# A trunk layer in float32: the head forms two products k tile by k tile, differences are taken of the raw input, and the K/V pair of the first gates comes last

## The chip, the cores and the metric

The kernel runs on one NeuronCore of one Trainium2 chip. TensorE (PE) multiplies, VectorE (DVE), ScalarE (ACT) and GpSimd (POOL) do elementwise work, and transfers are issued from the queues of SyncE (SP), ACT and POOL. The metric is the device time of one execution in microseconds. "Before" was timed in three executions, with a median of 1818.45 us (1814.23 to 1820.44), and profiled in a fourth.

## The reference

All data is float32: x is 2048 x 1024, one layer.

```python
shift, scale, gate = split(silu(c) @ w_ada + b_ada)      # 1024 each
u = x * (1 + scale) + shift                               # 2048 x 1024
q, k, v, a_gate, p_in, p_gate, m_a, m_p = split(u @ w_in) # 1024,128,128,1024,1024,1024,1024,1024
a = sliding_window_sink_attention(q, k, v, sinks, bias, mask) * silu(a_gate)   # 16 heads, 2 K/V heads, window 128
a = a @ w_attn_proj
p = group_linear(multiscale_causal_pool(p_in), w_pool_mix) * pool_scale * silu(p_gate)
p = p @ w_pool_proj
y = (sigmoid(m_a) * a + sigmoid(m_p) * p) @ w_out * (1 + gate)
out = layer_norm(2 ** 0.25 * x + y, ln_gain, ln_bias)
```

## The kernel before

**Numbers.** A float32 operand is split in two float32r parts: `hi` is a rounded copy made on ACT, `lo = src - hi` is made on DVE. A product of 128 x 128 by 128 x 512 is three matmuls (`mm3`: hi by hi, hi by lo, lo by hi). The third is the first to read the low part of the weights.

**Seven products instead of eight.** The large projections use a Winograd form of Strassen's scheme. For one half s of the sequence (1024 rows, in two chunks of 512), the moving operand u is cut in four blocks: B11 and B12 are the upper 512 features of the two chunks, B21 and B22 the lower 512. Seven operands, called sets, are kept in SBUF as four k tiles with hi and lo each: B11, T1 = B12 - B11, T2 = B22 - T1, B21, T3 = T2 - B11, B22, T4 = B21 - T2. A `Quad` is a pair of 128-column weight tiles; its `load` brings three quarters, and `sum1`, `mid` and `late` form the weight sums. It needs seven products of 12 matmuls each. `front` does B11 and T1 into two PSUM banks a and b; `back` does T2 (bank c) and B21 (onto a), then T3, B22 and T4. Each product but T4 takes its weights from `pair_split` (`first`, `second`, `third`), which writes two buffers out of the ring `w_set` of four. T4 uses `half_split`.

**Order.** `ring` walks over groups of two quads (one group has one). After each product `tick()` advances a position and runs the steps hung there in `hooks`; `steps(hooks, groups, start, todo)` hangs a list of steps at a tick counted through all groups (14 ticks to a group of two). Calls through `pe`, `act`, `dve`, `pool` and `sp` keep their place in the written order on their engine; calls on `nc.*` may be moved by the scheduler of the program.

**The head** (L1090 to L1228) loads w_ada and the first half of x and forms `mod` (shift and 1 + scale) k tile by k tile: `opening(k)` (16 one-column matmuls, a reduction over 128 x 1024 and an addition on DVE), `modulate_x(k)` on ACT. `middle(k)` makes B11 (k < 4) or B21, and the difference that becomes T1 or T2; `closing(k)` splits T1 or T2 one k tile later. `products(i)` does B11 and T1 of the first group per k tile. The T2 and B21 products of that group wait until `back`; their weights are split at the end of the head. The first group is the K/V pair and one quad of the gate `ag`.

**The first gates** (`first_phase`, L1230): 17 quads (K/V, then the gates ag, pg, ma, mp) in nine groups. The leftover sets T3, B22 and T4 are made at positions 0, 1 and 3 of group 0 (`rest`). Between the products four kinds of side work are hung: `fold_parts` (four times: w_pool_in folded with w_pool_mix, on PE, with weights split into two `w_set` buffers), `sums_to` (the sets of the second half of x, written to memory through `kept_parts`, which splits into tiles of the ring `c`), `gate_modulation`, and `turn` (V turned by PE). `spare` is a ring of two 128 x 1024 buffers, `c` one of five 128 x 512. The places of K (`kk`) and V (`vv`) are scratch in the head and then hold K and V. When the groups are done, `first_q` projects the first 128 columns of q (two times 24 matmuls), and attention begins.

## Time and profile before

| | |
|---|---|
| median of three executions | 1818.45 us |
| the profiled execution | 1809.75 us, its span 1808.0 us |
| PE busy | 1717.0 us (95%), 8248 matmuls |
| DVE, ACT, POOL busy | 1335.4, 905.5, 833.7 us |
| mean granted TensorE clock | 0.986 |

A row of the timeline is: start (us), length (us), engine, line, operation, output<-inputs, shape, count; in brackets the idle time before it and what ended it. All calls through the ordered engines carry line 55, so tile names tell them apart: `set_B` and `set_T` are the sets, `mm` and `lg` the PSUM banks for a, b and c, `t` the differences, `W` and `A` a quad's weights. Rows of waits are: who waited, for what, us in total, times, longest. PE's ends are modelled; starts are what is compared below.

### The profile page before, as it was taken

What the parts mean: (1) busy time and instruction counts of PE and PEld (TensorE: products, weight loads), DVE (VectorE), ACT (ScalarE), POOL (GpSimd) and SP (SyncE); (2) the same over time, 40 slices, a digit from 0 to 9 for tenths busy, and PEclk for the clock granted to TensorE, in tenths of its full rate; (3) what the DMA queues carried; (4) which work ended last, traced back from release to release, by engine and by line L of the source; (5) the groups of instructions that cost most, each with busy time, mean ns of one, the idle gap of its engine ahead of it and who ended that gap; (6) DMA issues with size and microseconds to landing.
All of it is one profiled execution on the core that took longest, in us unless ns stands there. A gap on an engine that the chain in (4) does not pass through costs nothing. (4 is left out here: it accounts for less than half of the span.)

```text
span 1808.0 us, 25116 instructions
## 1 busy us (share of the span) xinstructions
PE 1717.0 (95%) x8248; PEld 1430.8 (79%) x8248; DVE 1335.4 (74%) x2348; ACT 905.5 (50%) x1907; POOL 833.7 (46%) x700
## 2 busy tenths in 40 slices
PE   6799999999999999999999999999989999999996
PEld 6578787878888887777777888888868778877775
DVE  5977776655787777877766467777858897976887
ACT  4543434444777776444444367777724333423441
POOL 2134344440346567534434125456753773475442
PEclk9899999999999999999999999999999999999998
DMA  9255667756454557776776633543876575689442
GB/s 358 91 202 189 236 213 235 247 210 169 128 161 138 174 191 301 261 266 234 254 261 238 249 109 129 175 164 117 295 291 211 201 264 176 227 306 372 151 153 88
DMA packets 164002, 381.31 MB, mean 211 GB/s; under 512 B 19728, under 2 KB 23840, under 8 KB 163872
## 3 DMA queue, kind: packets, MB, share of 16 engines
q1 hardware_dynamic: 150528, 342.17, 54.4%
q0 software_dynamic: 10112, 33.06, 5.3%
q10 hardware_dynamic: 3232, 4.49, 0.9%
q8 instruction: 65, 1.06, 0.2%
q14 instruction: 65, 0.53, 0.1%
HBM read 244.35 MB, written 138.44 MB: 212 GB/s over the span
## 5 line engine op out<-in xcount | busy, mean ns | idle before, releaser
L55 PE MATMUL mm<-set_B,w_set 128*128 128x512 f32 x3240 | 799.9, 395 | 16.2 <-DVE w_set L131 14.7
L55 PEld LDWEIGHTS mm<-set_B,w_set 128*128 128x128 f32 x3240 | 602.6, 189 | 146.6 <-DVE w_set L131 20.7
L55 PE MATMUL lg<-set_T,w_set 128*128 128x512 f32 x2088 | 518.9, 398 | 40.1 <-DVE w_set L131 17.2
L55 PEld LDWEIGHTS lg<-set_T,w_set 128*128 128x128 f32 x2088 | 394.7, 191 | 140.1 <-DVE w_set L131 26.9
L131 DVE TENSOR_TENSOR w_set<-W,w_set 128x1024 fp32r<-128x1024 f32 x162 | 224.8, 1387 | 118.6 <-ACT w_set L315 108.2
L315 ACT CAST w_set<-W 128x1024 fp32r<-128x1024 f32 x162 | 169.5, 1049 | 265.3 <-PE mm L55 143.7
L55 PE MATMUL mm<-set_T,w_set 128*128 128x512 f32 x1080 | 266.2, 394 | 0.0
L55 PEld LDWEIGHTS mm<-set_T,w_set 128*128 128x128 f32 x1080 | 201.2, 189 | 41.7 <-DVE nxt L55 0.2
L283 POOL TENSOR_TENSOR W<-W,A 128x512 f32<-128x512 f32 x56 | 81.3, 1451 | 204.0 <-DVE w_set L131 40.0
L293 POOL TENSOR_TENSOR W<-W 128x512 f32<-128x512 f32 x56 | 82.9, 1481 | 158.4 <-DVE w_set L131 149.7
L287 POOL TENSOR_TENSOR W<-W 128x512 f32<-128x512 f32 x56 | 88.6, 1582 | 129.0 <-DVE w_set L131 104.1
L55 DVE TENSOR_TENSOR o<-pv,o 64x128 f32<-64x128 f32 x256 | 72.4, 283 | 92.6 <-ACT o L55 89.8
L55 ACT ACTIVATE L<-L,nm 128x257 f32<-128x257 f32 (+1 forms) x256 | 127.1, 498 | 8.4 <-DVE nm L55 3.2
L55 DVE TENSOR_TENSOR k_lo<-spare,k_hi 128x512 fp32r<-128x512 f32 x88 | 90.8, 1042 | 39.4 <-ACT k_hi L55 17.7
L55 DVE CUSTOM_DVE_ANT_0 L<-lg,bt,nsink 128x256 f32<-128x256 f32 (+1 forms) x256 | 111.5, 473 | 5.3 <-PE lg L55 1.3
L288 POOL TENSOR_TENSOR W<-W 128x512 f32<-128x512 f32 x56 | 91.1, 1627 | 19.7 <-DMA W<-in_win_dram 16.9
L55 POOL TENSOR_TENSOR w_set<-W,w_set 128x1024 fp32r<-128x1024 f32 x14 | 33.7, 2405 | 137.0 <-ACT w_set L55 96.5
L55 POOL TENSOR_TENSOR p<-nxt,pg 128x512 f32<-128x512 f32 x32 | 41.3, 1292 | 104.4 <-DVE sm L55 104.4
L55 ACT COPY o<-pv 64x256 f32<-64x256 f32 x128 | 47.2, 369 | 82.7 <-PE pv L55 80.4
L55 DVE TENSOR_TENSOR ptl<-pt,pth 128x512 fp32r<-128x512 f32 (+1 forms) x128 | 85.6, 669 | 1.7 <-ACT pth L55 1.6
L55 ACT CAST k_hi<-spare 128x512 fp32r<-128x512 f32 x88 | 53.3, 614 | 56.3 <-POOL spare L55 22.3
L55 PE MATMUL lg<-kk,qs 128*128 128x256 f32 (+1 forms) x512 | 80.5, 279 | 0.0
(206 smaller groups left out, 2429.9 us busy)
## 6 DMA issues: line engine op xcount, KB each, us to landing
W<-in_win_dram SPq DMA_DIRECT2D x68, 256.0 KB, 4.2
w_set<-wmix_d SPq DMA_DIRECT2D x32, 512.0 KB, 5.6
A<-in_win_dram SPq DMA_DIRECT2D x34, 256.0 KB, 4.4
W<-in_win_dram POOLq DMA_DIRECT2D x34, 256.0 KB, 3.6
ag_d<-sig SPq DMA_DIRECT2D x32, 256.0 KB, 3.5
pg_d<-sig SPq DMA_DIRECT2D x32, 256.0 KB, 3.2
ma_d<-sig SPq DMA_DIRECT2D x32, 256.0 KB, 3.8
mp_d<-sig SPq DMA_DIRECT2D x32, 256.0 KB, 4.0
```

The costliest lines, as they stand in the source:

```text
L55: return lambda *args, **kw: self.tc.keep_in_program_order(op(*args, **kw))
L131: engine.tensor_tensor(dst, src, as32(hi), ALU.subtract)
L283: e.tensor_tensor(self.w[:, 1, :], self.w[:, 2, :], self.a22, ALU.add)
L287: e.tensor_tensor(x[:, 1, :], x[:, 1, :], x[:, 0, :], ALU.subtract)
L288: e.tensor_tensor(x[:, 2, :], x[:, 0, :], x[:, 2, :], ALU.subtract)
L293: e.tensor_tensor(x[:, 0, :], x[:, 0, :], x[:, 1, :], ALU.subtract)
L315: a.copy(by_two(hi), raw)
```

## The change

1. `difference(k)` (k < 4) subtracts the raw halves of x ahead of the modulation. T1 is then scale times the difference: `closing` makes its hi by an ACT activation with a scale and its lo by a DVE `scalar_tensor_tensor`, and stores -scale in `sg`. T2's difference for k >= 4 is `t * (-scale) + B22`, one `scalar_tensor_tensor`.
2. `second_pair` and `more` do the T2 and B21 products of the first group inside the head, in parts as their k tiles come. `back` then gets the copy of bank a ready-made and leaves out both products.
3. T3 is made at the end of the head; B22 and T4 at positions 4 and 6 of group 0. `late` of the second quad moves to position 4.
4. In the first gates K/V goes from the first to the last group; the first group is two `ag` quads. V is turned at position 7 of the last group and between the two q projections. `place_kv` takes the places of K and V only then.
5. Until then these places are lent: folds split their weights into `room_k` and no longer into `w_set`; two of every three `kept_parts` split into `room_k`; `spare` takes every second pair from `room_v`.
6. Positions move: folds from 13, 41, 69, 92 to 11, 39, 67, 91, with one more tick between each split and its fold; `sums_to` of tile 0 from 1 to 4; `gate_modulation` by one tick, the last by five less.

```diff
         def __init__(self, name, **bufs):
-            self.name, self.bufs = name, bufs
+            self.name, self.bufs, self.turns = name, bufs, {}
         def __enter__(self):
             self.stack = ExitStack()
...
         def split(self):
             return wp.tile([P, D], F32R, tag="wset", bufs=4, name="w_set")
+        def turn_of(self, ring):
+            return next(self.turns[ring]) if ring in self.turns else None
+
         def spare(self, dt=F32):
+            room = self.turn_of("spare")
+            if room is not None:
+                return room
             return self.t.tile([P, D], dt, tag="spare", bufs=self.bufs["spare"], name="spare")
         def c(self, name="c", dt=F32, tag="c"):
...
         t = []
         def split():
-            t.extend(ph.c(n, F32R) for n in ("k_hi", "k_lo"))
+            at = ph.turn_of("parts")
+            if at:
+                t.extend(cols(rooms["k"], n + 2) for n in at)
+            else:
+                t.extend(ph.c(n, F32R) for n in ("k_hi", "k_lo"))
             act.copy(t[0], src())
             low(dve, t[1], src(), t[0])
...
     def back(ph, grp, opened, nxt, own, tick, b22_first=False):
         st = []
-        for q, (a, b, c, w) in zip(grp, opened):
-            u2, p5 = ph.p("u2"), ph.p("p5")
-            nc.scalar.copy(u2, a)
+        for q, (a, b, c, w, *copy) in zip(grp, opened):
+            u2 = copy[0] if copy else ph.p("u2")
+            p5 = ph.p("p5")
+            if not copy:
+                nc.scalar.copy(u2, a)
             if w is None:
                 w = pair_split(ph, q.second())
                 q.late()
...
             tick()
             nc.vector.tensor_tensor(u2, c, u2, ALU.add)
             nc.vector.tensor_tensor(p5, b, u2, ALU.add)
-            product(a, w[0], "B21")
+            if not copy:
+                product(a, w[0], "B21")
             tick()
             q.consume(ph, 0, 0, a)
             st.append((q, b, c, u2, p5))
...
         def consume(ph, mi, t, src):
             if mi == 0:
+                if s == 0 and t == 0:
+                    place_kv(ph)
                 take_k(s, t, src)
             else:
                 vt = ph.c("vt")
...
     def moving_u():
         return (sets["B11"], sets["B21"]), (sets["T2"], sets["B22"])
-    def first_q(ph, tick):
+    def first_q(ph, turn=None):
         raw, hi, lo = ph.spare(), ph.split(), ph.split()
         nc.sync.dma_start(raw, win[TQ])
...
         for us in moving_u():
             acc, part = projection(us)
             part((hi, lo), 0, KT)
+            if turn and not accs:
+                turn(1)
             accs.append(acc)
         return accs
...
                     m.append(wp.tile([P, CH], F32R, tag="A22", bufs=2, name=n))
                 act.copy(m[0], r[0])
                 low(dve, m[1], r[0], m[0])
-            w[:] = ph.split(), ph.split()
+            w[:] = (cols2(rooms["k"], n) for n in range(2))
             act.copy(w[0], r[1 + half])
             low(dve, w[1], r[1 + half], w[0])
...
             (0, lambda: fetch(0)),
             (1, lambda: fetch(1)),
             (2, lambda: split(0)),
-            (3, lambda: fold(0)),
-            (4, lambda: (keep(), split(1))),
-            (5, lambda: fold(1)),
-            (6, keep),
+            (4, lambda: fold(0)),
+            (5, lambda: (keep(), split(1))),
+            (7, lambda: fold(1)),
+            (8, keep),
         )
     def modulate(u, k):
...
     def gate_quads(s):
         kv, turn = kv_quad(s)
-        quads = [kv]
+        quads = [kv] if s else []
         for name, base, kind in (("ag", TAG, "silu"), ("pg", TPG, "scaled"), ("ma", TMA, ""), ("mp", TMP, "")):
             for m in range(0, KT, 2):
                 quads.append(gate_quad(s, name, base, m, kind))
-        groups = [quads[i : i + 2] for i in range(0, 14, 2)] + [quads[14:15], quads[15:17]]
-        return groups, turn
+        last = quads[15:] if s else [kv, quads[15]]
+        return [quads[i : i + 2] for i in range(0, 14, 2)] + [quads[14:15], last], turn
     def gate_modulation(ph, m, cb):
         wa = []
...
             b1, b2 = xs[k]
             if k < 4:
-                t = ts[k] = ph.p("t")
-                minus(t, b2, b1)
                 pool.dma_start(b12_d[k // 2, :, k % 2, :], b2)
             else:
-                minus(ts[k - 4], b2, ts[k - 4])
+                dve.scalar_tensor_tensor(ts[k - 4], ts[k - 4], sg[:, k - 4 : k - 3], b2, ALU.mult, ALU.add)
             parts("B11" if k < 4 else "B21", k % 4, b1)
+        def difference(k):
+
+            t = ts[k] = ph.p("t")
+            minus(t, xs[k][1], xs[k][0])
+
         def closing(k):
-            parts("T1" if k < 4 else "T2", k % 4, ts[k % 4])
+            if k >= 4:
+                parts("T2", k - 4, ts[k - 4])
+                return
+            hi, lo = sets["T1"][:, k, 0, :], sets["T1"][:, k, 1, :]
+            scale = mod[:, KT + k : KT + k + 1]
+            act.activation(hi, ts[k], AF.Copy, scale=scale)
+            dve.scalar_tensor_tensor(lo, ts[k], scale, as32(hi), ALU.mult, ALU.subtract)
+            act.activation(sg[:, k : k + 1], scale, AF.Copy, scale=-1.0)
         def rest_sums(i):
             minus(xs[i][0], ts[i], xs[i][0])
...
             if k < 2:
                 grp[k].load(ph, False, sp, None)
         opening(0)
+        difference(0)
         modulate_x(0)
         opening(1)
+        difference(1)
         middle(0)
         modulate_x(1)
+        def second_pair(x):
+
+            o, u2 = opened[x], ph.p("u2")
+            o[2:] = bank("lg"), pair_split(ph, grp[x].second(), act, dve), u2
+            act.copy(u2, o[0])
+
+        def more(x, name, i0, i1):
+            a, b, c, w, _ = opened[x]
+            if name == "T2":
+                product(c, w[1], name, True, i0, i1)
+            else:
+                product(a, w[0], name, False, i0, i1)
+
         for k in range(2, KT):
             opening(k)
+            if k < 4:
+                difference(k)
+            if k == 7:
+                second_pair(0)
             closing(k - 2)
             middle(k - 1)
             if k == 2:
...
                     q.sum1(dve)
                     starts.append(pair_split(ph, q.first(), act, dve))
             modulate_x(k)
-            if k in (3, 5):
-                grp[k // 2 - 1].mid(pool, dve)
+            if k in (3, 4):
+                grp[k - 3].mid(pool, dve)
             if 3 <= k < 7:
                 products(k - 3)
             if k > 5:
                 rest_sums(k - 6)
+        more(0, "T2", 0, 2)
+        more(0, "B21", 0, 3)
         closing(6)
+        second_pair(1)
+        more(1, "T2", 0, 2)
+        more(1, "B21", 0, 3)
         middle(7)
-        opened[0][3] = pair_split(ph, grp[0].second(), act, dve)
         closing(7)
-        opened[1][3] = pair_split(ph, grp[1].second(), act, dve)
-        for i in (3, 2):
+        for x in range(2):
+            more(x, "T2", 2, 4)
+            more(x, "B21", 3, 4)
+        for i in (2, 3):
             rest_sums(i)
-        for q in grp:
-            q.late(dve)
-        dve.tensor_scalar(nsink, nsink, -1.0, None, ALU.mult)
         late_sets(cp, "B22")
         late_sets(ph.t, "T3", "T4")
-        parts("T4", 1, xs[5][0])
+        for i in range(4):
+            parts("T3", i, xs[i][0])
+        grp[0].late(dve)
+        dve.tensor_scalar(nsink, nsink, -1.0, None, ALU.mult)
         rest = [
-            lambda name=name, src=src, ks=ks: [parts(name, i, src(i)) for i in ks]
-            for name, src, ks in (
-                ("T3", lambda i: xs[i][0], range(4)),
-                ("B22", lambda i: xs[4 + i][1], range(4)),
-                ("T4", lambda i: xs[4 + i][0], (0, 2, 3)),
-            )
+            lambda name=name, c=c: [parts(name, i, xs[4 + i][c]) for i in range(4)]
+            for name, c in (("B22", 1), ("T4", 0))
         ]
         return groups, turn, opened, cb, rest
...
             hooks.setdefault((group, pos), []).append(f)
         for g in range(4):
-            steps(hooks, groups, (13, 41, 69, 92)[g], fold_parts(ph, g))
-        for i in range(2):
-            at(0, (7, 10)[i], lambda i=i: turn(i))
+            steps(hooks, groups, (11, 39, 67, 91)[g], fold_parts(ph, g))
+        at(-1, 7, lambda: turn(0))
         for j in range(KT):
             at(3 + j // 2, 3 + 5 * (j % 2), lambda j=j: spread_bias(j))
         for i in range(4):
...
                 lambda x, r, ks=ks: modulate(x, ks[r]),
                 True,
             )
-            steps(hooks, groups, (1, 29, 57, 80)[i], todo)
+            steps(hooks, groups, (4, 29, 57, 80)[i], todo)
         for i in range(8):
-            steps(hooks, groups, 28 * (i // 2) + 20 + i % 2, gate_modulation(ph, 2 * KT + i, cb))
-        for n, f in zip((0, 1, 3), rest):
+            steps(hooks, groups, (21, 49, 77, 99)[i // 2] + i % 2, gate_modulation(ph, 2 * KT + i, cb))
+        at(0, 4, lambda: groups[0][1].late(dve))
+        for n, f in zip((4, 6), rest):
             at(0, n, f)
         for half in range(2):
             at(-1, 3 + half, lambda half=half: build(ph, "T2", half, b12_d))
-        return ring(ph, groups, opened, hooks, [], lambda tick: first_q(ph, tick))
+        return ring(ph, groups, opened, hooks, [], lambda tick: first_q(ph, turn))
     def second_phase(ph, opened, groups, turn):
         hooks = {(0, (8, 10)[i]): [lambda i=i: turn(i)] for i in range(2)}
...
                     steps(hooks, groups, 19 + 26.5 * i + 2.6 * n, resplit(ph, *halves_of.pop(0)))
         for half in range(2):
             hooks.setdefault((-1, 3 + half), []).append(lambda half=half: fill_set("T2", half, u1_d["B12"]))
-        return ring(ph, groups, opened, hooks, [], lambda tick: first_q(ph, tick), True)
+        return ring(ph, groups, opened, hooks, [], lambda tick: first_q(ph), True)
     def pairs(make):
         return [[make(m), make(m + 2)] for m in (0, 4)]
+
+    rooms = {}
+    kk = vv = None
+
+    def place_kv(ph):
+
+        nonlocal kk, vv
+        ph.turns.clear()
+        kk = kvp.tile([P, 2, 2, P + 2 * CH], F32R, tag="kk", name="kk")
+        vv = kvp.tile([P, 2 * NB + 1, 2, P], F32R, tag="vv", name="vv")
+
+    def cols2(t, n):
+        return t[:, n * D : (n + 1) * D]
     kv_stack = ExitStack()
     kvp = kv_stack.enter_context(tc.tile_pool(name="kvp", bufs=1))
...
     with Pools("g0", spare=2, p=4, c=5) as ph:
         started = head(ph)
-        kk = kvp.tile([P, 2, 2, P + 2 * CH], F32R, tag="kk", name="kk")
-        vv = kvp.tile([P, 2 * NB + 1, 2, P], F32R, tag="vv", name="vv")
+        rooms["k"] = kvp.tile([P, 4 * (P + 2 * CH)], F32R, tag="kk", name="room_k")
+        rooms["v"] = kvp.tile([P, 2 * (2 * NB + 1) * P], F32, tag="vv", name="room_v")
+        ph.turns["spare"] = cycle([None, None] + [cols2(rooms["v"], n) for n in range(2)])
+        ph.turns["parts"] = cycle([(2, 3), (4, 5), None])
         q0 = first_phase(ph, *started)
     with Pools("a0") as ph:
         gates1 = gate_quads(1)
```

1 line of the change is left out of this document (added).

## The prediction

> **What bounds the kernel now.** I read the page first, then PE's waits by stretch, then the timelines of PE, DVE and ACT in the stretches where PE waits.
>
> ```profile
> span 1808.0 us, 25116 instructions
> PE 1717.0 (95%) x8248; PEld 1430.8 (79%) x8248; DVE 1335.4 (74%) x2348; ACT 905.5 (50%) x1907; POOL 833.7 (46%) x700
> ```
>
> PE works through one fixed order of matmuls, so the change gains just what it takes out of PE's waits and slow clock. PE's waits from 24 to 76 us, then from 100 to 440 us:
>
> ```profile
> PE lg L55 <- DVE w_set L131: 6.3, 1, 6.3
> PE lg L55 <- ACT w_set L55: 3.8, 1, 3.8
> ...
> PE lg L55 <- DVE w_set L55: 1.2, 1, 1.2
> ...
> PE lg L55 <- ACT w_set L315: 7.7, 6, 1.9
> PE lg L55 <- DVE w_set L131: 3.8, 8, 0.5
> PE pv L55 <- DVE w_set L55: 0.8, 1, 0.8
> PE mm L55 <- DVE w_set L131: 0.7, 2, 0.4
> PE pv L55 <- ACT w_set L55: 0.6, 1, 0.6
> ```
>
> There are two places: the end of the head (11.3 us of waits) and the folds (most of 13.6 us). Around the head's end, by stretch (length, then PE, PEld, DVE, ACT, POOL busy, granted clock, DMA):
>
> ```profile
> 28.50:49.10 20.60, 20.57 (x114) 17.91 (x113) 19.17 (x35) 14.81 (x23) 2.16 (x4) 1.00 0.81 318
> 49.10:68.90 19.80, 14.82 (x50) 11.20 (x50) 19.72 (x33) 14.03 (x23) 0.00 (x0) 0.74 0.22 74
> ```
>
> To 49.1 PE is full; from there DVE is, 19.72 us of 19.80. PE and DVE from there on:
>
> ```profile
> 52.85 1.22 PE L55 MATMUL lg<-set_T,w_set 128*128 128x512 f32 x2 [3.77 <-ACT w_set L55]
> 55.27 4.63 PE L55 MATMUL lg<-set_T,w_set 128*128 128x512 f32 x10 [1.21 <-DVE w_set L55]
> ...
> 68.25 0.62 PE L55 MATMUL lg<-set_T,w_set 128*128 128x512 f32 x2
> 75.13 4.63 PE L55 MATMUL lg<-set_T,w_set 128*128 128x512 f32 x10 [6.26 <-DVE w_set L131]
> 79.57 3.57 PE L55 MATMUL mm<-set_B,w_set 128*128 128x512 f32 x12
> ...
> 107.49 2.60 PE L55 MATMUL lg<-set_T,w_set 128*128 128x512 f32 x10 [0.36 <-DVE w_set L131]
> ...
> 114.74 0.94 PE L55 MATMUL lg<-set_T,w_set 128*128 128x512 f32 x2 [1.93 <-ACT w_set L315]
> 116.00 3.71 PE L55 MATMUL lg<-set_T,w_set 128*128 128x512 f32 x10 [0.31 <-DVE w_set L131]
> ```
> ```profile
> 49.11 0.15 DVE L55 TENSOR_TENSOR mod<-mod,lg 128x1 f32<-128x1 f32 x1 [0.18 <-PE lg L55]
> ...
> 54.00 1.22 DVE L55 TENSOR_TENSOR w_set<-W,w_set 128x1024 fp32r<-128x1024 f32 x1
> 55.14 0.68 DVE L55 TENSOR_TENSOR set_T<-t,set_T 128x512 fp32r<-128x512 f32 x1
> 55.74 1.22 DVE L55 TENSOR_TENSOR w_set<-W,w_set 128x1024 fp32r<-128x1024 f32 x1
> ...
> 73.86 1.22 DVE L131 TENSOR_TENSOR w_set<-W,w_set 128x1024 fp32r<-128x1024 f32 x1
> ```
>
> The reader should see three things. The T2 products start only when their weights are split, 3.77 us after PE ran dry. T3's third matmul (75.13) waits for one DVE split, done at 75.08 because DVE has a queue of leftover sets and K copies ahead of it. And after such a gap ten matmuls take 4.63 us, where 2.60 is the full rate.
>
> **The change, part by part. T2 and B21 inside the head.** Start to start on DVE, a 512-wide operation takes 0.60 us and a weight split 1.14 (54.00, 55.14, 55.74). The four raw differences move ahead of the modulation one for one, into iterations where DVE has waits; in the last iterations PE is the limit (full to 49.1), so I leave `opening(7)` where it ends now, at 49.2. From there, in the new order, DVE does: split of the first quad's second weights (to 50.3), T2[1] low (50.9), the two of `middle(6)` (52.1), two leftover sums (53.3), T2[2] low (53.9), the second quad's weights (55.1), `middle(7)` (56.3), T2[3] low (56.9). PE can then run, at 0.23 us a matmul (2.75 from product to product of twelve; the 2.88 of a row holds the last one's tail): quad 0's first 15 matmuls of 24 between 49 and 53.6, waiting for DVE about 1 us; quad 1's first 15 from 55.1 to 58.1; the last 18 by 62.2. Now they end at 68.9.
>
> T3 comes next. DVE goes on with four leftover sums (59.3), four T3 lows (61.7) and `late` (62.3). The T3 weights follow on ACT and DVE; at the earliest at 64.5 (1.05 on ACT, 1.14 on DVE), at the latest behind the six 512-wide operations of `back` for both quads, 67.2. I take 65.4, behind one quad's three. So T3's third matmul moves from 75.1 to 65.4: **-9.7**. B22 and T4 (eight lows, 4.8 us) and the second `late` (0.6) now come later on DVE, under the T3 and B22 products of 2.75 us each. They are hidden by a narrow margin; without that cover they would cost up to 2.4 us each.
>
> The clock: the half rate after 75.13 costs 2.0 + 0.7 = 2.7 us now (4.63 against 2.60, 3.57 against 2.88 for twelve at full rate, a row below). After the change the gap ahead of T3 is some 3 us; its nearest row is 114.74, where 1.93 us of waiting cost (3.71 - 2.60) + 0.2 = 1.3. Net -1.4, of which I give back 1.0 for slow matmuls among the 48: **-0.4**. [...]
>
> The cost on DVE: `scalar_tensor_tensor` with a column as scalar, in SBUF:
>
> ```profile
> L611 DVE SCALAR_TENSOR_TENSOR wide<-wide,carry,wide 128x512 f32<-128x512 f32 x6 | 4.2, 745 | 0.4 <-POOL carry L607 0.4
> ```
>
> That is 0.06 us over a subtraction's 0.68, eight times 0.5 us, mostly while PE is full: nothing. ACT gains four scaled activations and four small ones, under 2 us, where it is busy 14.81 of 20.60 us. The `mid` of quad 1 and its POOL transfer go one iteration earlier; its split is 10 us off.
>
> **Folds without `w_set`.** A typical fold, ACT then PE:
>
> ```profile
> 201.74 1.05 ACT L55 CAST w_set<-spare 128x1024 fp32r<-128x1024 f32 x1 [2.15 <-DMA spare<-in_wpt_dram]
> ```
> ```profile
> 199.53 2.88 PE L55 MATMUL mm<-set_B,w_set 128*128 128x512 f32 x12
> 204.27 0.73 PE L55 MATMUL lg<-set_T,w_set 128*128 128x512 f32 x2 [1.86 <-ACT w_set L315]
> 205.53 2.56 PE L55 MATMUL lg<-set_T,w_set 128*128 128x512 f32 x10 [0.53 <-DVE w_set L131]
> ```
>
> The fold takes two of four buffers, so the next pair can be split only when the B21 product (199.53) is done, and PE waits for the whole split. Groups without a fold show waits of 0.3 to 0.5 us at most. Of the 13.6 us of waits from 100 to 440 us (7.7 + 3.8 + 0.8 + 0.7 + 0.6), four such small ones make 1.6; the eight halves of folds have 12.0, and the slow clock after 114.74 adds 1.3: 13.3 in all. With the folds in `room_k` each pair has two products (5.5 us) to hide 2.2 us of split, a slack of 3.3. What is late next is ACT itself, which stands in order behind the fold's two loads (first two rows, ACT's waits from 75 to 440 us):
>
> ```profile
> ACT w_set L55 <- DMA spare<-in_wpt_dram: 7.6, 4, 3.1
> ACT mhi L55 <- DMA mr<-in_mix_dram: 6.8, 4, 2.5
> ACT k_hi L55 <- DMA u_T_split<-k_hi: 6.6, 2, 4.3
> ```
>
> That is 3.6 us a fold, against 3.3 of slack; the longer `spare` lets the loads go two ticks earlier past fewer stores on SP. I keep 2.0 back: **-11.3**, with bounds -13.3 and -6.
>
> **The last fold** moves one position, behind the T3 product of the single-quad group. Its `mlo` and `mhi` hold the two `A` places that the next group's quads load into:
>
> ```profile
> 379.53 0.86 SPq L277 DMA_DIRECT2D A<-in_win_dram  x2
> ```
> ```profile
> 385.96 1.33 DVE L131 TENSOR_TENSOR w_set<-W,w_set 128x1024 fp32r<-128x1024 f32 x1 [2.86 <-ACT w_set L315]
> ```
>
> From that issue to the finished split are 7.7 us, and now 8.2 us of products cover them (T3, B22, T4); then only two, 5.5. SP's stores behind the load wait too. Price 2.2, less the two matmuls that need no low part: **+1.7** (0 to 4; a gain is excluded, PE's work is the same).
>
> **K/V last.** The same instructions move. In the last group `take_k` puts four casts and four subtractions (some 0.6 us each) per chunk ahead of a pair split with 3.3 us of slack, and V's turn lies between the two q projections (5.5 us each). The nearest row is K/V in the first gates of the second half, where K is taken on the way to this wait:
>
> ```profile
> 740.95 2.60 PE L55 MATMUL mm<-set_B,w_set 128*128 128x512 f32 x10 [0.26 <-DVE w_set L131]
> ```
>
> I take **+0.7** (-0.5, since V's turn leaves a stretch where DVE is full, to 5, all of `take_k` exposed). The lent `room_v` is priced at nothing: no place in it is asked for again before its last user is four ticks past. The pairs in `room_k` come round after three splits, some two ticks or 5.5 us, about what a split and its store take (the longest wait for a store is 4.3, the `k_hi` row); that is part of the 2.0 kept back. The other moved positions change no order on PE beyond the folds', and I price them at nothing.
>
> **Sum**: -9.7 - 0.4 - 11.3 + 1.7 + 0.7 = -19.0 us. Against the profiled execution, 1809.75, that is 1790.8. That execution is 0.5% below the median of 1818.45; on the median's scale, which I predict, **1799**.
>
> **The rivals.** *The folds' ACT waits stay* (0.14): if the loads land no earlier, 3.6 us a fold exceed the slack, and half of 11.3 goes: 1805.
>
> *Half clock through the head's products* (0.11): PE now gets T2 and B21 in crumbs. At the rate of 55.27 (0.44 us a matmul) 48 take 21 us, from 49.4 to 70.5, and T3 gains 4.6, not 9.7: 1804. The stretch 49.10 to 68.90 with its clock of 0.74 speaks for it; that it had 5 us of gaps and not 2 speaks against. [...]
>
> *K/V's chain holds up attention* (0.07): in the head's group, where DVE was full, K and V took 41 us, from 63.0 to 104.3:
>
> ```profile
> 63.01 0.58 ACT L650 CAST kk<-mm 64x512 fp32r<-64x512 f32 x1 [0.98 <-PE mm L55]
> ...
> 103.65 0.74 DVE L131 TENSOR_TENSOR vv<-pt,vv 128x256 fp32r<-128x256 f32 x2
> ```
>
> At the end eight products and two q projections, 33 us, follow the first K. If it were as slow there, 8 us would be exposed: 1806. The row at 740.95 speaks against it.
>
> *One room, one lock*, the slower side (0.12, and 0.07 that it only eats up the gain; this also stands for a cost of its kind that I don't see): if uses of a lent tile wait for each other though they touch different columns, 22 of the 32 splits of `sums_to` wait on ACT for the store before them, 3.3 us each by the `k_hi` row, 73 us in all. About half would lie within the slack; I estimate 30 us on PE, and the folds' gain is lost with it. What is left of the gain is 7.7, so it decides from 8 us on; worked out, 1841. Against it: a load into the third column block of `head_B` was issued while PE still read the first:
>
> ```profile
> 8.07 0.44 SPq L55 DMA_DIRECT2D head_B<-in_wadat_dram  x1
> ```
> ```profile
> 7.82 3.55 PE L55 MATMUL pv<-ct,head_B 128*128 128x1 f32 x16 [7.82 <-DMA head_B<-in_wadat_dram]
> ```
>
> **The numbers.** Forecast 0.49, rivals as given. The forecast's own range adds its bounds: 1791 to 1810. The range, 1788 to 1813, adds what runs differ by and leaves out the last rival's 0.19. A measurement tells apart about 0.3%, 5.4 us: the forecast and the first three rivals are faster (0.81), the last gives 0.07 within and 0.12 slower.
>
> **What would show it.** T2 matmuls should start near 49 to 50 us, all 48 end by 62 to 65, and T3's third matmul start near 65. PE's waits for `w_set` between 100 and 440 us should fall from 13.6 to some 4. Attention should begin some 19 us earlier, and the rest keep its length. I am wrong if waits reappear there under another name: DVE ahead of B22 or T4, `A` ahead of the last group, ACT behind a fold's load, or the clock below 0.9 between 50 and 80 us.

## The result and the profile after

The kernel after takes 1810.94 us (median of nine executions, 1805.66 to 1816.67); before, beside it, the median of nine was 1818.45 us (1811.51 to 1820.44). The ratio is 0.9964, with a 95% interval of 0.9947 to 0.9980: faster by 7.5 us between the medians, 6.5 us by the ratio. The prediction was 19 us. So the sign was right, and more than half of the gain is missing. The profiled execution after took 1813.58 us, span 1811.8 us; the one before, 1809.75 us, lies 0.5% below its median. The two spans can't be set against each other, and I compare the same products in both.

The page's first lines after, and PE's waits after from 24 to 76 us and from 100 to 440 us (who waited, for what, us in total, times, longest):

```profile
span 1811.8 us, 25114 instructions
PE 1716.2 (95%) x8248; PEld 1428.6 (79%) x8248; DVE 1344.2 (74%) x2348; ACT 905.7 (50%) x1911; POOL 841.8 (46%) x700
```
```profile
PE lg L56 <- DVE w_set L132: 2.5, 1, 2.5
PE lg L56 <- ACT w_set L326: 1.6, 1, 1.6
...
PE lg L56 <- DVE w_set L56: 0.8, 1, 0.8
...
PE mm L56 <- DVE w_set L132: 5.8, 6, 1.4
PE lg L56 <- ACT w_set L326: 4.0, 1, 4.0
PE lg L56 <- DVE p L400: 1.5, 1, 1.5
PE lg L56 <- DVE w_set L132: 1.4, 2, 1.0
PE mm L56 <- ACT w_set L326: 1.4, 1, 1.4
```

Ahead of T3, 11.3 us of waits became 4.9. Between 100 and 440 us, 13.6 became 14.1: the same sum under other names. The folds' waits (six for ACT with `lg`, and those of `pv`) are all gone; in their place stand seven waits of `mm` (`set_B` products), three small ones of `lg`, and one of 4.0 us that has no like before. PE's timeline after shows where:

```profile
48.52 0.72 PE L56 MATMUL lg<-set_T,w_set 128*128 128x512 f32 x2
...
63.90 0.73 PE L56 MATMUL lg<-set_T,w_set 128*128 128x512 f32 x2 [1.62 <-ACT w_set L326]
67.12 4.05 PE L56 MATMUL lg<-set_T,w_set 128*128 128x512 f32 x10 [2.49 <-DVE w_set L132]
...
82.31 5.33 PE L56 MATMUL lg<-set_T,w_set 128*128 128x512 f32 x22 [2.41 <-DVE w_set L132]
...
89.10 2.56 PE L56 MATMUL mm<-set_B,w_set 128*128 128x512 f32 x10 [0.99 <-DVE w_set L132]
...
95.62 2.60 PE L56 MATMUL mm<-set_B,w_set 128*128 128x512 f32 x10 [0.79 <-DVE w_set L132]
...
100.78 2.88 PE L56 MATMUL lg<-set_T,w_set 128*128 128x512 f32 x12
...
144.29 2.56 PE L56 MATMUL mm<-set_B,w_set 128*128 128x512 f32 x10 [1.15 <-DVE w_set L132]
...
374.62 0.73 PE L56 MATMUL mm<-set_B,w_set 128*128 128x512 f32 x2 [1.42 <-ACT w_set L326]
375.98 2.57 PE L56 MATMUL mm<-set_B,w_set 128*128 128x512 f32 x10 [0.63 <-DVE w_set L132]
...
396.60 5.47 PE L56 MATMUL lg<-set_T,w_set 128*128 128x512 f32 x12 [4.01 <-ACT w_set L326]
...
421.65 2.71 PE L56 MATMUL mm<-set_B,w_set 128*128 128x512 f32 x11
```

T3's third matmul comes 8.0 us earlier (67.12 against 75.13). The first T2 product of the next group, at 100.78, comes 5.7 us earlier (106.51 before): the waits at 82.31, 89.10 and 95.62, 4.2 us together, took 2.3 net back. It isn't more in part because V's turn, 0.8 us of PE's work and a wait of 0.4 (at 88.52 and 97.81 before), now comes behind this point. From there to T4 of the eighth group the gain grows by 9.0, to 14.7 us; the last fold (374.62, 375.98) takes 2.6, the wait at 396.60 with its twelve matmuls at half rate 6.4, and V's turn 0.4. At the q projections (421.65 against 426.93) 5.3 us are left.

What DVE and POOL do ahead of the waits in group 0, and DVE further on, after:

```profile
65.86 1.22 DVE L132 TENSOR_TENSOR w_set<-W,w_set 128x1024 fp32r<-128x1024 f32 x1
...
75.27 1.78 DVE L56 TENSOR_TENSOR set_T<-head_kk,set_T 128x512 fp32r<-128x512 f32 x1
...
78.67 2.38 DVE L56 TENSOR_TENSOR set_T<-head_vv,set_T 128x512 fp32r<-128x512 f32 x2
...
81.58 1.28 DVE L132 TENSOR_TENSOR w_set<-A,w_set 128x512 fp32r<-128x512 f32 x2
...
83.38 1.52 DVE L56 TENSOR_SCALAR spare<-spare,mod 128x1024 f32<-128x1024 f32 x2
...
128.44 0.69 DVE L408 TENSOR_TENSOR c<-mm,u 128x512 f32<-128x512 f32 x1 [6.09 <-PE mm L56]
...
137.76 2.32 DVE L56 CUSTOM_DVE_ANT_0 spare<-spare,cb,mod 128x1024 f32<-128x1024 f32 x1
...
140.62 1.27 DVE L56 CUSTOM_DVE_ANT_0 spare<-spare,cb,mod 128x1024 f32<-128x1024 f32 x1
```
```profile
73.02 1.78 POOL L294 TENSOR_TENSOR W<-W,A 128x512 f32<-128x512 f32 x1 [32.54 <-DMA A<-in_win_dram]
...
78.28 1.62 POOL L299 TENSOR_TENSOR W<-W 128x512 f32<-128x512 f32 x1
```

T3's weights are split at 65.86, behind all six operations of `back`: the late end that the prediction had worked out. T4's (81.58) come behind T4's own four subtractions, which take up to 1.8 us and not 0.6 while POOL sums the next group's weights. At 128.44 DVE stands 6 us ahead of the first sum that follows a B22 product (tile `c`, L408), and the two reductions of `gate_modulation` now follow each other at 137.76 and 140.62, ahead of the weight split that PE waits for at 144.29.

For the wait at 396.60: first the issues and ACT's wait after, then the stretch from 384 to 396 us (length, PE, PEld, DVE, ACT, POOL busy, granted clock, DMA share, GB/s), then the transfers issued from 380 to 400 us (packets of ACT's queue; KB each and median us to landing), and the usual time from the page:

```profile
382.67 0.40 ACTq L1317 DMA_DIRECT2D gate_d<-mod  x1
384.07 0.57 POOL L300 DMA_DIRECT2D W<-in_win_dram  x1 [0.30 <-POOL W L298]
...
395.51 1.04 ACT L326 CAST w_set<-W 128x1024 fp32r<-128x1024 f32 x1 [9.55 <-DMA W<-in_win_dram]
```
```profile
384.00:396.00 12.00, 8.48 (x36) 6.32 (x35) 1.23 (x1) 1.54 (x2) 1.85 (x2) 0.94 0.23 25
```
```profile
q10 hardware_dynamic: 1040, 0.00, 2.9%
...
W<-in_win_dram POOLq DMA_DIRECT2D x2, 256.0 KB, 7.1
gate_d<-mod ACTq DMA_DIRECT2D x1, 4.0 KB, 9.3
```
```profile
W<-in_win_dram POOLq DMA_DIRECT2D x34, 256.0 KB, 4.1
```

`mod` is stored to `gate_d` as 1024 single elements (4 KB in over a thousand packets). The last quarter of the next quad's weights, issued 1.4 us later, was there only at 395.5, 11.4 us after its issue, where 4.1 is usual; in these 12 us the DMA engines moved 25 GB/s. In the profile before, the same transfer was issued later, where only a DVE operation waited for it (5.5 us, at 425.00):

```profile
411.34 0.43 ACTq L1268 DMA_DIRECT2D gate_d<-mod  x1
```

It came earlier because the change moves the last pair of `gate_modulation` five positions ahead, and the store is a call that goes out as soon as `mod` is complete.

### The profile page after: what moved, and what is told of

Read it like the earlier page. It is cut to its first block, busy times and chain, and to the rows that moved or that the text cites. A ratio compares the mean times of both kernels' runs of the same rounds, so it can differ in the third digit from the quotient of the medians.

```text
span 1811.8 us, 25114 instructions
## 1 busy us (share of the span) xinstructions
PE 1716.2 (95%) x8248; PEld 1428.6 (79%) x8248; DVE 1344.2 (74%) x2348; ACT 905.7 (50%) x1911; POOL 841.8 (46%) x700
## 5 line engine op out<-in xcount | busy, mean ns | idle before, releaser
L298 POOL TENSOR_TENSOR W<-W 128x512 f32<-128x512 f32 x56 | 90.5, 1616 | 142.2 <-DVE w_set L132 110.2
L304 POOL TENSOR_TENSOR W<-W 128x512 f32<-128x512 f32 x56 | 84.6, 1512 | 148.3 <-DVE w_set L132 140.7
L299 POOL TENSOR_TENSOR W<-W 128x512 f32<-128x512 f32 x56 | 93.4, 1667 | 19.9 <-DMA W<-in_win_dram 16.8
L56 DVE TENSOR_TENSOR k_lo<-spare,k_hi 128x512 fp32r<-128x512 f32 x61 | 64.6, 1065 | 31.0 <-ACT k_hi L56 14.8
L56 ACT ACTIVATE L<-L,sm 128x256 f32<-128x256 f32 (+1 forms) x128 | 64.3, 502 | 31.4 <-DVE sm L56 31.2
```

The costliest lines, as they stand in the source:

```text
L56: return lambda *args, **kw: self.tc.keep_in_program_order(op(*args, **kw))
L298: e.tensor_tensor(x[:, 1, :], x[:, 1, :], x[:, 0, :], ALU.subtract)
L299: e.tensor_tensor(x[:, 2, :], x[:, 0, :], x[:, 2, :], ALU.subtract)
L304: e.tensor_tensor(x[:, 0, :], x[:, 0, :], x[:, 1, :], ALU.subtract)
```

## The experiments

One execution of these kernels tells little of the time (before's lay between 1809.8 and 1824.4). So the experiments are read at two points of PE's order: T2 of the second group (106.51 us before, 100.78 after) and the start of the q projections (426.93 and 421.65). Three of them are also timed. Experiments 1 and 11 are one kernel profiled twice, and agree to 0.1 us at the first point (100.94, 101.03) and to 0.4 at the second (415.15, 414.78). What the clock does behind a wait is less steady: ten matmuls behind the last fold took 2.57 us after (375.98), 4.63 in experiment 1 and 4.06 in experiment 11, behind waits of 2.0 to 2.3 us. So a difference of up to 3 us at the q projections counts only together with a wait that is named.

**1. The store of `gate` later.** Is the wait at 396.60 the store's doing, or late work on ACT and DVE? It is moved into attention (n counts its steps).

```diff
-            nc.scalar.dma_start(gate_d.rearrange("k p -> p k"), mod[:, 16:24], allow_slow_non_contiguous=True)
...
+            if s == 0 and n == 20:
+                act.dma_start(gate_d.rearrange("k p -> p k"), mod[:, 16:24], allow_slow_non_contiguous=True)
```

> The changed kernel, but the transfer of the gate row (gate_d<-mod, 1024 pieces of 4 bytes) is issued in attention and no longer between the two quads' last weight quarters of the last group. Theory: that transfer is what held the second quarter (issued at 384.07, used at 395.51). Then PE's wait of 4.01 us and the product at half rate behind it (5.47 us for 2.88) go, and the q projections start near 415 us where they start at 421.65 now. Rival: the K/V work on ACT and DVE in the last group makes that wait; then the wait stays and they start at 421 to 422.

The wait is gone and the q projections start at 415.15, 6.5 us earlier; from 384 to 396 us PE is busy for all 12.00 us at a granted clock of 1.00 (8.48 us and 0.94 after). The theory holds. (Up to the product ahead of that wait this kernel is 0.7 us behind, 387.26 against 386.54, so the store is worth 7.2 us here. The 6.4 above are against the kernel before, which has a wait of 0.5 us of its own at this place.) The profile of this kernel also names what DVE waits for in the row of 128.44 above: the fold's result, which is being stored out of the same ring `c`.

```profile
127.76 0.69 DVE L408 TENSOR_TENSOR c<-mm,u 128x512 f32<-128x512 f32 x1 [5.64 <-DMA wmix_d<-st_hi]
```

**2. `gate_modulation` at its old positions.**

```diff
-            steps(hooks, groups, (21, 49, 77, 99)[i // 2] + i % 2, gate_modulation(ph, 2 * KT + i, cb))
+            steps(hooks, groups, 28 * (i // 2) + 20 + i % 2, gate_modulation(ph, 2 * KT + i, cb))
```

> The changed kernel with gate_modulation at its old positions (20, 48, 76, 104). Theory: its two reductions on DVE now come back to back ahead of the second quad's first split, and make the waits of 1.15 us at 142.5 and 1.35 us at 229.6; these go (2.5 us). With the last pair later, the gate row's transfer also leaves the place between the last weight quarters, 6.6 us: q projections near 412.6. Rival: the leftover work of group 0 and the sums make these waits and the K/V work the last one: 421 to 422, waits as they are.

The last group's wait goes here too (0.6 us is left), but the q projections start at 418.31, not at 412.6. The reductions meet other work; one of them, in DVE's row, now stands ahead of the `p` sum that PE waits for (PE's row):

```profile
133.07 2.28 DVE L56 CUSTOM_DVE_ANT_0 spare<-spare,cb,mod 128x1024 f32<-128x1024 f32 x1
...
136.11 4.38 PE L56 MATMUL lg<-set_T,w_set 128*128 128x512 f32 x12 [3.73 <-DVE p L400]
```

Half right: what the new positions cost in the last group, they had gained elsewhere.

**3. Folds split into `w_set` again.**

```diff
-            w[:] = (cols2(rooms["k"], n) for n in range(2))
+            w[:] = ph.split(), ph.split()
```

> The changed kernel with the folds' weights split into w_set again, all else as changed. Theory: the lent room is worth what the eight waits at the folds were in the kernel before, 12 us of waits: the q projections move from 421.65 to 431 to 435. Rival: with one more tick between split and fold the ring would do as well; then under 3 us, 422 to 425.

The q projections start at 431.25, 9.6 us later than after, and the old waits are back in the groups from 100 to 440 us (the longest of the eight is the store's):

```profile
PE lg L56 <- ACT w_set L326: 10.8, 8, 3.7
```

PE's waits in this stretch add up to 20.2 us, 6.1 more than after. With the spacing of the folds as it is after the change, the lent place is worth 9.6 us. This part of the prediction holds.

**4. The head's products back behind the head.**

```diff
-        more(0, "T2", 0, 2)
-        more(0, "B21", 0, 3)
...
-            more(x, "B21", 3, 4)
+        opened[0][3] = pair_split(ph, grp[0].second(), act, dve)
...
+        opened[1][3] = pair_split(ph, grp[1].second(), act, dve)
```

> The changed kernel with the first group's T2 and B21 products behind the head again; T3 stays in the head, K/V last. Theory: these products in the head are worth the 8 us that T3's third matmul came earlier: it starts at 74 to 76 us again (67.1 now), and the q projections at 428 to 430. Rival: group 0 then waits for DVE in any case, and B22 and T4 are ready while PE is still busy: T3 at 70 to 72 us, and the q projections lose under 3 us, 422 to 425.

T2 of the second group at 101.03 (100.78 after), the q projections at 420.88 (421.65). T3 came earlier than either expectation had it: it starts at 67.71 and doesn't wait. DVE gets to T4's split at 81.49 (81.58 after), and so PE reaches T4 at the same time with and without the products in the head:

```profile
67.71 2.93 PE L56 MATMUL lg<-set_T,w_set 128*128 128x512 f32 x12
...
82.22 6.95 PE L56 MATMUL lg<-set_T,w_set 128*128 128x512 f32 x22 [2.81 <-DVE w_set L132]
```

The rival holds: in this kernel the head's products are worth nothing.

**5. Before, with K/V last and nothing else.**

```diff
-        quads = [kv]
+        quads = [kv] if s else []
...
+        last = quads[15:] if s else [kv, quads[15]]
...
-            at(0, (7, 10)[i], lambda i=i: turn(i))
+        at(-1, 7, lambda: turn(0))
...
+            if turn and not accs:
+                turn(1)
```

> The kernel before with K/V moved to the last group and nothing else: no lent places, no products in the head, the leftover sets as they were. Theory (DVE is the bound from the end of the head to T4 of group 0, and K/V's own work on DVE there is only part of it): three K subtractions stand ahead of T3's split in the profile before (67.88, 69.92, 71.94), some 2 us, so T3's third matmul comes at 73 and not 75.1, T4's first product at 87 and not 88.9, and the q projections start 1 to 2 us earlier, at 425 to 426 (426.9 before). Rival (taking K/V out of group 0 is the whole of what the change gained there): T4 at 82 to 83, q projections at 420 to 421.

```profile
69.37 2.58 PE L55 MATMUL lg<-set_T,w_set 128*128 128x512 f32 x10 [0.63 <-DVE w_set L131]
...
100.70 2.88 PE L55 MATMUL lg<-set_T,w_set 128*128 128x512 f32 x12
...
109.81 5.68 PE L55 MATMUL lg<-set_T,w_set 128*128 128x512 f32 x12 [3.51 <-ACT w_set L315]
```

Neither: T3's third matmul comes at 69.37 (75.13 before), T4 starts at 84.26, between the two, and T2 of the second group at 100.70. That is 5.8 us earlier than before, as much as the kernel after has at this point. My expectation counted only the K subtractions in front of T3's split. On DVE, K (first row) and V had 9.2 us of the profile before between 60 and 110 us (length; PE, PEld, DVE, ACT busy; granted clock, DMA share, GB/s):

```profile
60.00:110.00 50.00, 0.00 (x0) 0.00 (x0) 6.30 (x9) 4.80 (x8) 0.93 0.46 156
...
60.00:110.00 50.00, 0.00 (x0) 0.00 (x0) 2.87 (x5) 1.18 (x2) 0.93 0.46 156
```

The `ag` quad in their place takes 3.1 us more there (its products into `sig`: 6.94 against 3.81), so DVE is relieved of some 6 us. T3's split runs at 68.10 and not 73.86. Of these 5.8 us, the four K subtractions that stood ahead of it are 2.7; most of the rest is order, since a `p` sum and three subtractions of T3 now come behind that split. And 1.2 of the 5.8 us at T2 are V's turn with its wait, which moved on PE itself. The next fold, still in `w_set`, then waits longer (109.81, 3.5 us and half rate), and at the q projections 2.0 us are left (424.96).

**6. The next group's weights later (no verdict),** with the store of `gate` late. Moving the loads one or two products later in `back` was to bring POOL's sums behind T4's subtractions.

```diff
+            n = len(opened[0]) > 4 and (2 if q is nxt[0] else 1)
-            defer(1, lambda: q.load(ph, own, e=None))
-            defer(3, lambda: q.sum1(nc.gpsimd))
+            defer(1 + n, lambda: q.load(ph, own, e=None))
+            defer(3 + (n > 0), lambda: q.sum1(nc.gpsimd))
```

> The kernel after with the transfer of gate late (as in the first experiment), and in group 0 the loads of the next group's weights asked for one or two products later, so that POOL's four sums come behind T4's subtractions on DVE. Theory (DVE's five operations from 74.6 to 81.0 take 6.4 us and not 3.0 because POOL works beside them, 73.0 to 79.9): they take 3 us again, T4's first product starts at 79.5 to 80 (82.5 in the first experiment), and the q projections 2 to 3 us earlier, at 412 to 413 (415.15). Rival (DVE is slow there for another reason, or has too much to do anyway): T4 at 82 to 83 and the q projections at 415 or later.

These loads are calls that the scheduler may move, and POOL's sums still began at 72.3. T4 at 82.58 and the q projections at 414.36 tell nothing of the theory; experiment 10 asks again.

**7. Folds at their old positions**, still in the lent place, with the store of `gate` late.

```diff
-            (4, lambda: fold(0)),
-            (5, lambda: (keep(), split(1))),
-            (7, lambda: fold(1)),
-            (8, keep),
+            (3, lambda: fold(0)),
+            (4, lambda: (keep(), split(1))),
+            (5, lambda: fold(1)),
+            (6, keep),
...
-            steps(hooks, groups, (11, 39, 67, 91)[g], fold_parts(ph, g))
+            steps(hooks, groups, (13, 41, 69, 92)[g], fold_parts(ph, g))
```

> The kernel after with the transfer of gate late, and the folds at their old positions with their old spacing (starts 13, 41, 69, 92; split and fold in neighbouring positions), still split into the lent place. Theory (the new waits at 128 and 134 and the two ahead of the last group come from the moved fold steps): the 2.05 us ahead of the last group and the 1.5 at 134 go, the q projections start at 411 to 412 (415.15 in the first experiment). Rival (the wider spacing is what hides the folds' loads and splits): PE waits for the folds' splits, 0.5 to 1.5 us in each of eight halves, and the q projections start at 417 or later.

The waits ahead of the last group go, but the q projections start at 419.26, 4.1 us later than in experiment 1: PE now waits for the folds' splits, 4.5 us in four waits.

```profile
358.88 0.39 PE L56 MATMUL pv<-mhi,room_k 128*128 128x256 f32 x1 [1.89 <-ACT room_k L56]
```

The rival holds, with one limit: positions and spacing were moved together. One of the two, and by these waits the spacing, is part of what makes the lent place pay.

**8. T4's subtractions one position earlier (with the store of `gate` late), and five repairs at once.**

```diff
-        for n, f in zip((4, 6), rest):
+        for n, f in zip((4, 5), rest):
```

The second kernel has this, the store of `gate` late, and three more: the reductions of a pair three positions apart, the second half of a fold stored out of the lent place, and the last fold's second half one position earlier.

```diff
-            steps(hooks, groups, (21, 49, 77, 99)[i // 2] + i % 2, gate_modulation(ph, 2 * KT + i, cb))
+            steps(hooks, groups, (21, 49, 77, 99)[i // 2] + 3 * (i % 2), gate_modulation(ph, 2 * KT + i, cb))
...
-                st = [ph.c(n, F32R).rearrange("p (m e d) -> p m e d", m=2, e=2) for n in ("st_hi", "st_lo")]
+                st = [cols(rooms["k"], 2 * n + i) if lent else ph.c(x, F32R) for i, x in enumerate(("st_hi", "st_lo"))]
+                st = [x.rearrange("p (m e d) -> p m e d", m=2, e=2) for x in st]
...
-            (7, lambda: fold(1)),
-            (8, keep),
+            (7 - (g == 3), lambda: fold(1)),
+            (8 - (g == 3), lambda: keep(True)),
```

> The kernel after with the transfer of gate late, and the splits of T4 in group 0 one position earlier (5 and not 6): the same operations on DVE, put where it idles (1.13 us at 71.2 and 0.31 at 73.9 in the profile after) and ahead of POOL's sums, which begin at 73.0. Theory (T4's first product waits for DVE's queue, which is full of that stage's own work and stretched beside POOL): T4's first product starts at 80 to 81 (82.48 in the first experiment), and the q projections 1.5 to 2.5 us earlier than 415.15, at 412.7 to 413.7. Rival (T4 waits for something else, its A operand or the bank): 82.5, and 415.

> The kernel after with five repairs together: transfer of gate late; T4's splits at position 5; the two reductions of gate_modulation three positions apart; the second half of each fold stores out of the lent place and not out of the ring c; the last fold's second half ahead of the T3 product of the single-quad group. Theory (each new wait between 80 and 400 us has the cause named for it): T4 at 80 to 81, the waits at 128 and 134 (0.2 to 1.5), at 144 and 230 (1.1 to 1.4 each) and ahead of the last group (2.3) go, and the q projections start at 408 to 409, where the prediction had them (426.9 - 19 = 407.9). Rival (they move elsewhere, DVE being near its limit in these groups): 412 or later.

T4's place alone: its first product starts at 81.51, later than the 80 to 81 expected, its second then waits 3.2 us, and T2 of the second group comes at 102.67, 1.7 us later than in experiment 1. The q projections start at 413.25, as expected in number but not by this road: experiment 1 had slow matmuls behind the last fold (4.63 us for ten at 373.78, 3.76 for the next twelve, 2.9 us over full rate), and this kernel had none there. That is luck. With all five repairs the q projections start at 408.24, inside the 408 to 409 expected, though T4's part again goes the wrong way:

```profile
88.81 4.63 PE L56 MATMUL lg<-set_T,w_set 128*128 128x512 f32 x10 [3.22 <-DVE w_set L132]
```

**9. The four repairs without T4's place**, timed (as the second kernel above, without the first edit).

> The five repairs without the one that failed: T4's splits of group 0 go back to position 6. Theory: the q projections start at 407 to 408.5 (408.24 with all five, of which T4's place cost about as much at 88 us as it gave at 81), that is 13 to 14 us earlier than in the kernel after, and the median of the time is 8 to 13 us below the kernel after's, 1798 to 1803, a ratio of 0.989 to 0.992 to before, if the phases behind keep at least two thirds of it. Rival (what is gained ahead of attention is lost again in the phases behind, where loads and stores bound the starts): 1805 to 1811.

1794.80 us (1792.92 to 1796.46), ratio to before 0.9877 (0.9862 to 0.9892): 22 us faster than before. The q projections start at 403.82, earlier than I expected, since T4's place had cost 4 us and not 1 (T2 of the second group at 100.72 against 104.78). All of PE's waits from 100 to 440 us:

```profile
PE mm L56 <- DVE w_set L132: 1.8, 2, 1.2
```

Which of the three repairs besides the store brought how much wasn't tried apart.

**10. The next group's loads held back on SP's queue**, with the four repairs, timed.

```diff
-            defer(1, lambda: q.load(ph, own, e=None))
-            defer(3, lambda: q.sum1(nc.gpsimd))
+            g0 = len(opened[0]) > 4
+            n = (4 if q is nxt[0] else 2) if g0 else 1
+            defer(n, lambda: q.load(ph, own, sp if g0 else nc.sync, None))
+            defer(n + 1 if g0 else 3, lambda: q.sum1(nc.gpsimd))
```

> The kernel with the four repairs, and in group 0 the six loads of the next group's weights put on SP's queue behind the stores that wait for T3's and B22's results, so that POOL's four sums start some 5 us later (78 and 83 and not 73.0). Theory (DVE's subtractions take 1.7 to 2.4 us and not 0.6 to 0.7 while POOL sums): between 74.5 and 78 they take 0.6 again, T4's first product starts at 79.5 to 80.5 (82.5 with the four repairs), the q projections 1.5 to 2.5 us earlier than there. Rival (DVE's load alone holds T4 up): T4 at 82 or later, and the later weights cost a wait ahead of B11 of the next group.

DVE, POOL and PE of this kernel:

```profile
76.55 1.28 DVE L56 TENSOR_TENSOR set_T<-head_vv,set_T 128x512 fp32r<-128x512 f32 x2
...
80.16 3.51 DVE L56 TENSOR_SCALAR spare<-spare,mod 128x1024 f32<-128x1024 f32 x2
```
```profile
79.01 2.39 POOL L294 TENSOR_TENSOR W<-W,A 128x512 f32<-128x512 f32 x1 [38.53 <-DMA A<-in_win_dram]
```
```profile
79.47 5.67 PE L56 MATMUL lg<-set_T,w_set 128*128 128x512 f32 x24
...
89.45 4.63 PE L56 MATMUL mm<-set_B,w_set 128*128 128x512 f32 x10 [3.85 <-DVE w_set L132]
```

With POOL's first sum at 79.01 (72.45 without this edit), T4's subtractions take 0.6 us each again and T4 starts at 79.47 with no wait. So the long subtractions were POOL's doing: beside POOL operations of 1.6 to 1.8 us, a subtraction of 0.68 (75.34 here) took 1.78 (75.27 after). But other work is hit in its place: the two operations at 80.16 take 3.51 and not 1.52, two more at 84.19 take 2.87 and not 1.28, B11 of the next group waits 3.85 us and restarts at half rate, and T2 comes at 102.41, 1.7 us later than without the edit. The time is 1796.44 us (1791.29 to 1801.08), ratio 0.9889 (0.9872 to 0.9907), not to be told from experiment 9. Are the later weights to blame, as the rival has it? DVE has no idle time from 74.14 to 96.5, and it does the split that B11 waits for at 88.19, though ACT's half of it was done at 82.5; without the edit it did it at 87.81. So DVE's total bounds this stage in both places of POOL's sums.

**11. Experiment 1 timed.**

> The first experiment's kernel again (the kernel after with the transfer of gate late, nothing else), for its time and a second profile. Theory (what attention gains in its start, 6.5 us, reaches the end): a ratio of 0.993 to before, 0.991 to 0.995, and the q projections again at 415. Rival (the phases behind give it back): 0.996, as the kernel after.

1806.74 us (1800.60 to 1810.42), ratio 0.9935 (0.9914 to 0.9956), q projections at 414.78. The interval reaches up to the rival's 0.996, but the whole row of timed kernels shows that what is gained at the q projections is gained at the end (last column: one minus the ratio, times 1817):

| | q projections | earlier by | ratio to before | us by the ratio |
|---|---|---|---|---|
| after | 421.65 | 5.3 | 0.9964 | 6.5 |
| store late (11) | 414.78 | 12.2 | 0.9935 | 11.8 |
| loads held (10) | 405.46 | 21.5 | 0.9889 | 20.2 |
| four repairs (9) | 403.82 | 23.1 | 0.9877 | 22.3 |

In the single profile after, part of the 5.3 us looks lost behind attention (T2 of the second gates comes 2.6 earlier, 696.14 against 698.76). That is one execution against one; the timed runs speak for the whole.

## Why the prediction was right or wrong

**T3 from 75.1 to 65.4, and what followed from it (-9.7 and -0.4): wrong in what pays for it.** T3's third matmul came at 67.12, the late bound, 1.7 us off. The 48 matmuls ran from 48.52 to 62.3, as forecast. The step that failed is "B22 and T4 now come later on DVE, hidden by a narrow margin": the cover was gone (2.41 us ahead of T4, then 0.99 and 0.79), and at T2 of the second group 5.7 us were left of 10.1. More than that, experiment 4 shows that these 5.7 us don't come from the products, nor do the 8.0 at T3: without the products in the head T3's third matmul comes only 1 us later (some 68.2, an estimate: two matmuls of 0.23 us behind 67.71), and the B22 product behind it is 0.5 us earlier (70.48 against 71.01). K/V last alone gives 5.8 us at T2 of the second group (experiment 5). I had charged PE's gaps of 49 to 75 us to the order of the work, though the row of that stretch (DVE 19.72 of 19.80 us) said that DVE was the bound. Products moved on PE don't shorten DVE's queue; taking K and V out of it brought T3's split forward. That the 5.7 us after and the 5.8 of experiment 5 are one and the same gain is argued from DVE's rows and not shown: neither the products nor the kernel after were tried with K/V still first.

**The clock there (-0.4): about right.** PE did not crawl: the 48 matmuls took 13.8 us, not the 21 of the rival, at a granted clock of 0.88 from 48.52 to 62.30. Ten matmuls after the gap took 4.05 us (clock 0.60 from 67.12 to 71.20), 1.45 over full rate, where I had 1.3 from the row at 114.74. This loss came behind two gaps of 1.62 and 2.49 us, with two matmuls between. A single gap of 2.41 us at 82.31 had no loss behind it (22 matmuls in 5.33 us, clock 1.00); one of 2.81 in experiment 4 did (22 in 6.95).

**Folds (-11.3): right in mechanism, too large by 2.3.** The waits at the folds' eight halves are gone, and experiment 3 gives the place's worth as 9.6. From T2 of the second group to the eighth group 9.0 were gained. I had kept back 2.0 for ACT behind the folds' loads; what came instead is DVE: the sum behind B22 waiting for a place in `c` (128.44), reductions back to back ahead of a split (1.15 at 144, 1.35 at 231).

**Last fold (+1.7): right**, measured 2.6, of which 2.05 are the waits at 374.62 and 375.98. The chain is the one forecast: `A` is asked for at 367.60, behind the fold, and POOL's sum starts with it at 372.22. It could have been up to 2.9 us more by the clock, as experiment 1 shows.

**K/V last (+0.7): wrong at the other end of the move.** In the last group it cost 0.4. That "the same instructions move" overlooked what they had cost where they came from, and a gain that they alone can give (5.8 us, 1.2 of it V's turn moved on PE) stood under the head's name.

**Moved positions ("price at nothing"): wrong, 6.4 us.** I priced the order on PE. The reductions of `gate_modulation` end in a transfer on another queue; as they ended earlier, it went out beside a weight load that PE needed. This is the largest single error, and experiments 1 and 11 confirm it.

Together: 4.4 in group 0, 2.3 in the folds, 0.9 for the last fold and 6.4 for the store, less 0.3 for K/V, are the 13.7 us between the 19.0 forecast and the 5.3 found at the q projections. That the median lies inside the stated range, 1788 to 1813, is no credit to the mechanism: its slow end was added up from folds that gain only 6 and K/V that costs 5, and the runs showed 9.0 and 0.4. Of the rivals, the folds' ACT waits did not stay, K/V did not hold up attention, and the one lock did not show: from 75 to 440 us ACT waited 0.8 us in all for a store out of `room_k`, where that rival had 73. The signs named at the end of the prediction were the right ones: DVE ahead of T4 did show.

## What to carry to other kernels

When an engine's row says that it is full in a stretch, count a change there by what it takes out of that engine's queue; the 48 matmuls moved on the engine that waits gave T3 about 1 us here and the product behind it nothing. Of a step that is moved, follow what its last result sets off, on every queue: a transfer of 4 KB in single elements cost more than half of what the rest of the change had brought (6.4 of 11.7 us). And repair what a profile shows after a change before judging it: with four small repairs the same idea is worth 22 us and not 7. Whether some of these repairs would also speed up the kernel before wasn't tried.

## What the runs showed of the hardware

- A store of 1024 single elements took 9.3 us (13.6 before), with 1040 packets on its queue from 380 to 400 us, and held up a load of 256 KB on another queue to 11.4 us, where 4.1 is usual. With the store moved away (experiment 1), PE's wait of 4.01 us for that load's weights was gone.
- A subtraction on DVE of 0.68 us (75.34 in experiment 10) took 1.78 beside sums on POOL (75.27 after), and two scalings took 3.51 and not 1.52 (80.16 in experiment 10). Putting POOL's work elsewhere moved the loss here and didn't remove it (experiment 10).
